# FFN products on h itself from the fourth f-tile on, in place of scale * x with two shift columns

## The chip, the cores and the metric

The kernel runs on one core of one Trainium2 chip. The metric is the device time of one execution in microseconds (us); lower is better. Engines are named as in the profile: PE (matmul), PEld (its weight loads), DVE, ACT, POOL, and SP, which issues DMAs.

## The reference, cut to what matters

The model is a two-layer backbone over 128 context tokens and 256 latent tokens (together T = 384 columns). Each layer has two SwiGLU feed-forward blocks (FFNs) around a token mixer, so there are four FFNs. Width D is 1024, hidden width is 2816.

```
h = modulate(rmsnorm(x, norm_g), shift, scale)      # y * (1 + scale) + shift
x = x + 0.5 * gate * ((silu(h @ wg) * (h @ wu)) @ wd)
```

Shift, scale and gate are vectors of D values, one set for the context tokens and one for the latent ones.

## The kernel before, in words

Activations lie transposed: the 128 partitions hold a slice of the width, the free axis holds the 384 tokens. xT holds x as 8 such slices (k = 0 to 7).

Every product of the FFN is done in three passes (`mm3`): weights and activations are each split into a high part (rounded to fp32r) and a low part (the rest), and high*high, high*low and low*high are added up in one PSUM tile. `loadw` loads a weight tile by a DMA that SP issues, ACT casts the high part wh (L575), DVE subtracts for the low part wl (L576).

`ffn` has two stages. In the gate/up stage a loop over 22 f-tiles (f = 0 to 21) multiplies each of two weight tiles (gate, then up) with the 8 slices of the activation: 2 x 8 x 3 = 48 matmuls for one f-tile. The activation is not h. RMS norm needs the sum of squares over the whole width, and so as not to wait for it, the kernel multiplies with scale * x (tiles xh and xl, written by `norm_step` while the stage before still runs) and appends the two shift vectors as columns 384 and 385. So xh and xl have T + 2 = 386 columns, and each gate/up matmul streams 386. `norm_end` (L560) adds up the squares after f = 0 and forms r, one over the root, on DVE and ACT; r is finished by the DVE instruction on L527. The epilogue of an f-tile (L625 to L634) then copies the two shift columns of the product out of PSUM (L628), multiplies gate and up by r (L629), applies silu with the shift product as bias, once for each token segment (L631), adds the other shift product and multiplies (L632), and writes the high and low part of the result to row f of gh (L633, ACT) and gl (L634, DVE). In the down stage 8 x 22 x 3 matmuls for the 8 output slices read gh and gl with 384 columns, and `residual` adds to xT.

In the first three FFNs some matmuls for the modulation vectors ("fills", L482) stand between the f-tiles; the fourth has none.

The instructions of an engine run in a fixed order, which a planner sets when the kernel is built: at each point it takes, among those it holds to be ready, the one that stands first in the program. Buffers of a pool are reused in turn. The mixer's function `normed` forms h in the same way as the change does (POOL multiplies by r, ACT scales and shifts, ACT casts, DVE subtracts), for the products of the mixer; its helper records everything on L267.

Of the kernel before, what the change touches and what calls it, by code (L numbers as in the profile page):

```python
# [10 lines left out]
F32 = mybir.dt.float32  # L11
F32R = mybir.dt.float32r
AF = mybir.ActivationFunctionType
ALU = mybir.AluOpType
# [3 lines left out]
KD = D // 128  # L18
TP = 128
TS = 256  # L20
T = TP + TS
SEGS = ((0, TP), (TP, T))
DEPTH = 2
DFF = 2816
NF = DFF // 128
# [286 lines left out]
class Kernel:  # L312
# [235 lines left out]
    def norm_step(self, k):  # L548
# [8 lines left out]
        if k:  # L557
            (nc.vector if k == KD - 1 else nc.gpsimd).tensor_tensor(out=self.acc, in0=self.acc, in1=sq, op=ALU.add)

    def norm_end(self):  # L560
        if self.r is not None:
            return
        ps = self.psm()[:, :T]
        self.nc.tensor.matmul(ps, self.k(K_ONE), self.acc, start=True, stop=True)
        self.r = self.rsqrt([ps], [128, T], 1.0 / D, self.eps[:, 0:1], lambda i, n: self.xp.tile([128, T], F32, tag=f"nr{n}", name="nr"))[0]
# [29 lines left out]
    def ffn(self, l, which, mods, nxt):  # L595
        nc, tc, I = self.nc, self.tc, self.I
        sub = 2 * which
        wg, wu, wd = I['ffn_gate'][l, which], I['ffn_up'][l, which], I['ffn_down'][l, which]
        with ExitStack() as st:

            tp = st.enter_context(tc.tile_pool(name="ft", bufs=1, reuse_waits="tile"))
            wp = st.enter_context(tc.tile_pool(name="fw", bufs=FW, reuse_waits="tile"))
            gp = st.enter_context(tc.tile_pool(name="fg", bufs=1, reuse_waits="tile"))
            gh = gp.tile([128, NF, T], F32R, name="gh")
            gl = gp.tile([128, NF, T], F32R, name="gl")
            fills = chain.from_iterable(self.ada(x, i, tp) for x, i in mods)
            steps = (KD + 1) * len(mods)
            if l == sub == 0:
                rest = self.rest(tp)
                next(rest)  # L610
                fills = chain(fills, rest)
                steps += 3
            xh, xl = self.xh, self.xl

            for f in range(NF):
                cols = slice(f * 128, (f + 1) * 128)
                ws = [self.loadw(w[:, cols].rearrange("(k p) f -> p k f", p=128), [128, KD, 128], wp, 1 if f else 4) for w in (wg, wu)]
                gu = [self.psm() for w in ws]

                for i, k in sorted(((i, k) for i in range(2) for k in range(KD)), key=lambda x: f == 0 and x[1] == KD - 1):  # L620
                    self.mm3(gu[i][:, 0:T + 2], ws[i][0][:, k, :], ws[i][1][:, k, :], xh[:, k, :], xl[:, k, :], k == 0, k == KD - 1)
                self.norm_end()
                for _ in range(steps * (f + 1) // NF - steps * f // NF):
                    next(fills, None)
                b = tp.tile([128, 4], F32, tag="fb", bufs=2, name="fb")  # L625
                g, u = (tp.tile([128, T], F32, tag=n, bufs=2, name=n) for n in ("fs", "fa"))
                for i, x in enumerate((g, u)):
                    nc.vector.tensor_copy(out=b[:, 2 * i:2 * i + 2], in_=gu[i][:, T:T + 2])  # L628
                    nc.vector.tensor_mul(out=x, in0=gu[i][:, 0:T], in1=self.r)  # L629
                for c, (x, y) in enumerate(SEGS):  # L630
                    nc.scalar.activation(out=g[:, x:y], in_=g[:, x:y], func=AF.Silu, bias=b[:, c:c + 1])  # L631
                    nc.vector.scalar_tensor_tensor(out=u[:, x:y], in0=u[:, x:y], scalar=b[:, 2 + c:3 + c], in1=g[:, x:y], op0=ALU.add, op1=ALU.mult)  # L632
                nc.scalar.copy(out=gh[:, f, :], in_=u)  # L633
                nc.vector.tensor_sub(out=gl[:, f, :], in0=u, in1=gh[:, f, :])  # L634
            assert next(fills, self) is self
            G = self.adac[l, 3 * sub + 2]
            if nxt:
                self.norm_begin(nxt)
            else:
                self.final_begin()  # L640
            for m in range(KD):
                ps = self.psd()[:, :T]
                for k0 in range(0, NF, KD):
                    n = min(KD, NF - k0)
                    d = self.loadw(wd[k0 * 128:(k0 + n) * 128, m * 128:(m + 1) * 128].rearrange("(k p) f -> p k f", p=128), [128, n, 128], wp)
                    for k in range(n):
                        kk = k0 + k
                        self.mm3(ps, d[0][:, k, :], d[1][:, k, :], gh[:, kk, :], gl[:, kk, :], kk == 0, kk == NF - 1)
                self.residual(m, ps, G)
                (self.norm_step if nxt else self.final_step)(m)  # L650
# [1477 lines left out]
```

## Time and profile before

| | |
|---|---|
| median of 3 runs | 2522.77 us (2519.91 to 2525.49) |
| the profiled execution, its time | 2523.17 us |
| its span, first to last instruction | 2521.4 us |
| PE busy | 2394.0 us (95%) |
| DVE busy | 1581.8 us (63%) |
| ACT busy | 1127.0 us (45%) |
| POOL busy | 489.5 us (19%) |
| granted PE clock, mean | 0.979 of 2.4 GHz |

A row of the timeline gives the start in us from the start of the span, the duration, the engine, the line, the operation, the tile written and the tiles read, and the shapes. Matmul durations overlap; how fast PE goes is the distance from start to start. A row of a stretch gives the busy time of each engine in it, the number of instructions, then the granted clock, the busy share of the DMA engines and GB/s.

### The profile page before, as it was taken

To read this page: it belongs to the slowest core of one execution; us is meant where nothing else is said; L and a number is where in the kernel's file an instruction comes from. 1 tells how busy PE (TensorE), PEld (TensorE's weight loads), DVE (VectorE), ACT (ScalarE), POOL (GpSimd) and SP (SyncE) were. 2 spreads that over 40 slices of the span, in tenths; PEclk is the share of its full clock that TensorE was granted. 3 is DMA by queue.
4 is the path that set the end of the run, shared out by engine and by line. 5 is a ranking of instruction groups with operands and counts; after the bars stand their busy time and mean duration, and the time that the engine had idled before them with its cause. 6 is when DMAs were issued, how large, how long until landed. Compare 5 with 4: busy or idle time off the path is not lost.

```text
span 2521.4 us, 51149 instructions
## 1 busy us (share of the span) xinstructions
PE 2394.0 (95%) x20545; PEld 2168.4 (86%) x20545; DVE 1581.8 (63%) x3466; ACT 1127.0 (45%) x2303; POOL 489.5 (19%) x667
## 2 busy tenths in 40 slices
PE   6999999999999879999999999999999997899998
PEld 4999998778888669999999999978788885799998
DVE  3544468778658886555445544786885587865543
ACT  3333346555446544333343333754544654443332
POOL 3000024323104541000000001441231345210000
PEclk8999999999999989999999999999999998999999
DMA  9876454323355126554557754533333541444442
GB/s 309 270 250 212 121 152 108 82 76 92 92 151 151 51 82 204 170 176 143 160 177 226 220 172 129 142 97 82 84 96 97 142 148 30 146 126 126 125 116 86
DMA packets 501677, 354.31 MB, mean 141 GB/s; under 512 B 40035, under 2 KB 479985, under 8 KB 500927
## 3 DMA queue, kind: packets, MB, share of 16 engines
q1 hardware_dynamic: 496288, 337.44, 45.5%
q0 software_dynamic: 3680, 6.18, 1.2%
q10 hardware_dynamic: 1471, 7.41, 0.8%
q8 instruction: 162, 2.65, 0.4%
q14 instruction: 76, 0.62, 0.1%
HBM read 326.59 MB, written 24.38 MB: 139 GB/s over the span
## 4 chain that ended last, share of the span: by engine, by line
PE 77%; DVE 12%; ACT 3%; issue 3%; POOL 3%; DMA 2%; SPq 0%; ACTq 0%; POOLq 0%; DVEq 0%
PE psd L267 17%; PE psm L267 12%; PE psm L586 10%; PE psm L588 10%; PE psm L587 10%; PE psd L586 5%; PE psd L587 5%; PE psd L588 5%; PE pss L482 3%; DVE wl L267 2%; POOL kb L267 1%; DVE gD L267 1%; DVE M L267 1%; ACT L267 1%; DMA xT<-xd 1%
## 5 line engine op out<-in xcount | busy, mean ns | idle before, releaser
L575 ACT CAST wh<-wraw 128x1024 fp32r<-128x1024 f32 (+2 forms) x296 | 279.9, 956 | 674.4 <-PE psm L587 264.4
L586 PE MATMUL psm<-xh,wh 128*128 128x386 f32 x1408 | 486.1, 345 | 1.0 <-DVE xh L545 0.6
L588 PE MATMUL psm<-xh,wl 128*128 128x386 f32 x1408 | 478.4, 340 | 1.0 <-DVE wl L576 1.0
L587 PE MATMUL psm<-xl,wh 128*128 128x386 f32 x1408 | 478.1, 340 | 0.0
L576 DVE TENSOR_TENSOR wl<-wraw,wh 128x1024 fp32r<-128x1024 f32 (+2 forms) x296 | 325.6, 1106 | 184.6 <-ACT wh L575 184.4
L267 PE MATMUL psd<-mhh,wh 128*128 128x384 f32 x848 | 295.9, 350 | 6.2 <-DVE sb L267 5.4
L267 PE MATMUL psd<-mhl,wh 128*128 128x384 f32 x848 | 297.3, 351 | 2.7 <-DVE mhl L267 2.7
L267 PE MATMUL psd<-mhh,wl 128*128 128x384 f32 x848 | 297.3, 351 | 0.0
L586 PEld LDWEIGHTS psm<-xh,wh 128*128 128x128 f32 x1408 | 266.1, 189 | 27.3 <-issue 16.9
L267 DVE TENSOR_TENSOR wl<-wraw,wh 128x512 fp32r<-128x512 f32 x324 | 244.7, 766 | 70.2 <-ACT wh L267 67.5
L588 PEld LDWEIGHTS psm<-xh,wl 128*128 128x128 f32 x1408 | 265.3, 188 | 2.1 <-DVE wl L576 2.1
L587 PEld LDWEIGHTS psm<-xl,wh 128*128 128x128 f32 x1408 | 266.8, 190 | 0.1
L267 ACT CAST wh<-wraw 128x512 fp32r<-128x512 f32 x324 | 191.7, 615 | 133.8 <-PE psd L267 111.0
L628 DVE COPY fb<-psm 128x2 f32<-128x2 f32 x176 | 27.9, 159 | 343.4 <-PE psm L588 343.4
L587 PE MATMUL psd<-gl,wh 128*128 128x384 f32 x704 | 235.9, 335 | 0.0
L588 PE MATMUL psd<-gh,wl 128*128 128x384 f32 x704 | 235.9, 335 | 0.0
L586 PE MATMUL psd<-gh,wh 128*128 128x384 f32 x704 | 235.6, 335 | 0.0
L267 PEld LDWEIGHTS psd<-mhh,wh 128*128 128x128 f32 x848 | 161.5, 191 | 21.1 <-issue 11.7
L267 PEld LDWEIGHTS psd<-mhl,wh 128*128 128x128 f32 x848 | 161.3, 190 | 14.9 <-issue 5.9
L267 PEld LDWEIGHTS psd<-mhh,wl 128*128 128x128 f32 x848 | 161.4, 190 | 8.8 <-issue 2.4
L267 PE MATMUL psd<-ob,wh 128*128 128x384 f32 x384 | 110.1, 364 | 24.8 <-ACT ob L267 17.3
L586 PEld LDWEIGHTS psd<-gh,wh 128*128 128x128 f32 x704 | 132.2, 188 | 0.9 <-issue 0.4
(434 smaller groups left out, 4297.3 us busy)
## 6 DMA issues: line engine op xcount, KB each, us to landing
wada<-in_w_ada_dram SPq DMA_DIRECT2D x144, 512.0 KB, 4.5
wraw<-in_w_in_dram SPq DMA_DIRECT2D x112, 512.0 KB, 3.9
wraw<-in_ffn_gate_dram SPq DMA_DIRECT2D x88, 512.0 KB, 4.7
wraw<-in_ffn_up_dram SPq DMA_DIRECT2D x88, 512.0 KB, 3.9
wraw<-in_ffn_down_dram SPq DMA_DIRECT2D x64, 512.0 KB, 3.9
wraw<-in_ffn_down_dram SPq DMA_DIRECT2D x32, 384.0 KB, 3.4
gate<-sa SPq DMA_DIRECT2D x48, 192.0 KB, 3.5
gate<-gate SPq DMA_DIRECT2D x48, 192.0 KB, 2.5
```

What stands on the lines that cost most here:

```text
L267: r = f(*a, **k)
L482: nc.tensor.matmul(ps[32 * j:32 * j + 32, 0:256], self.cs[:, kk, :], w[:, 256 * j:256 * j + 256], start=(kk == 0), stop=(kk == KD - 1), ti ...
L575: nc.scalar.copy(out=h[:, x], in_=r[:, x])
L576: nc.vector.tensor_sub(out=lo[:, x], in0=r[:, x], in1=h[:, x])
L586: nc.tensor.matmul(ps, wh, xh, start=first, stop=False)
L587: nc.tensor.matmul(ps, wh, xl, start=False, stop=False)
L588: nc.tensor.matmul(ps, wl, xh, start=False, stop=last)
L628: nc.vector.tensor_copy(out=b[:, 2 * i:2 * i + 2], in_=gu[i][:, T:T + 2])
```

## The change

For f = 0 to 2 the loop is as before. In the epilogues of f = 0 and f = 1 the new function `norm_h` forms h for four slices each: POOL multiplies xT by r into a buffer nu (two buffers), ACT applies scale and shift in place (two instructions, one for each token segment), ACT casts the high part, DVE subtracts for the low part. The results th and tl are put into rows 14 to 21 of gh and gl, which the loop does not write before f = 14. From f = 3 on the matmuls read h with 384 columns: th and tl for f = 3 to 11; from f = 12 on columns 0 to 383 of xh and xl, into which ACT copies one slice of th and tl in each of the epilogues of f = 3 to 10. The epilogue from f = 3 on is a silu straight from PSUM, one multiply, and the two writes of gh and gl.

```diff
+    def norm_h(self, k, pool, hh, hl):
+        nc, (l, sub) = self.nc, self.ls
+        A, S = self.adac[l, 3 * sub + 1], self.adac[l, 3 * sub]
+        u = pool.tile([128, T], F32, tag="nu", bufs=2, name="nu")
+        nc.gpsimd.tensor_mul(out=u, in0=self.xT[:, k, :], in1=self.r)
+        for c, (a, b) in enumerate(SEGS):
+            nc.scalar.activation(out=u[:, a:b], in_=u[:, a:b], func=AF.Identity, scale=A[:, k, c:c + 1], bias=S[:, k, c:c + 1])
+        nc.scalar.copy(out=hh[:, k, :], in_=u)
+        nc.vector.tensor_sub(out=hl[:, k, :], in0=u, in1=hh[:, k, :])
...
-            xh, xl = self.xh, self.xl
+            F1, F2 = 3, 12
+            x, n = (self.xh, self.xl), T + 2
+            th, tl = gh[:, NF - KD:, :], gl[:, NF - KD:, :]
...
+                if f == F1:
+                    x, n = (th, tl), T
+                elif f == F2:
+                    x = self.xh[:, :, 0:T], self.xl[:, :, 0:T]
...
-                    self.mm3(gu[i][:, 0:T + 2], ws[i][0][:, k, :], ws[i][1][:, k, :], xh[:, k, :], xl[:, k, :], k == 0, k == KD - 1)
+                    self.mm3(gu[i][:, 0:n], ws[i][0][:, k, :], ws[i][1][:, k, :], x[0][:, k, :], x[1][:, k, :], k == 0, k == KD - 1)
...
+                if f < F1:
...
+                else:
+                    nc.scalar.activation(out=g, in_=gu[0][:, 0:T], func=AF.Silu)
+                    nc.vector.tensor_mul(out=u, in0=gu[1][:, 0:T], in1=g)
                 nc.scalar.copy(out=gh[:, f, :], in_=u)
                 nc.vector.tensor_sub(out=gl[:, f, :], in0=u, in1=gh[:, f, :])
+                if f < 2:
+                    for k in range(4 * f, 4 * f + 4):
+                        self.norm_h(k, tp, th, tl)
+                elif F1 <= f < F1 + KD:
+                    k = f - F1
+                    nc.scalar.copy(out=self.xh[:, k, 0:T], in_=th[:, k, :])
+                    nc.scalar.copy(out=self.xl[:, k, 0:T], in_=tl[:, k, :])
```

## Rows read from the trace of the kernel before

**Rows 1.** The page: busy time by engine; the chain that ended last, by engine.

```profile
PE 2394.0 (95%) x20545; PEld 2168.4 (86%) x20545; DVE 1581.8 (63%) x3466; ACT 1127.0 (45%) x2303; POOL 489.5 (19%) x667
...
PE 77%; DVE 12%; ACT 3%; issue 3%; POOL 3%; DMA 2%; SPq 0%; ACTq 0%; POOLq 0%; DVEq 0%
```

**Rows 2.** Stretches: gate/up from f = 3 (fourth FFN), f = 2 (first FFN).

```profile
2253.80:2406.60 152.80, 152.80 (x865) 152.80 (x864) 86.81 (x162) 59.67 (x90) 0.00 (x0) 1.00 0.42 124
62.60:262.30 199.70, 199.70 (x1376) 181.38 (x1375) 100.28 (x205) 66.32 (x101) 0.00 (x0) 1.00 0.76 237
```

**Rows 3.** Timeline of PE, gate/up stage of the fourth FFN.

```profile
2330.19 0.34 PE L586 MATMUL psm<-xh,wh 128*128 128x386 f32 x1
...
2332.33 0.34 PE L586 MATMUL psm<-xh,wh 128*128 128x386 f32 x1
...
2333.22 0.33 PE L588 MATMUL psm<-xh,wl 128*128 128x386 f32 x1
...
2334.26 0.34 PE L588 MATMUL psm<-xh,wl 128*128 128x386 f32 x1
```

**Rows 4.** Timeline of PE, down stage of the fourth FFN.

```profile
2452.78 0.33 PE L586 MATMUL psd<-gh,wh 128*128 128x384 f32 x1
...
2454.86 0.33 PE L586 MATMUL psd<-gh,wh 128*128 128x384 f32 x1
```

**Rows 5.** Timeline of DVE: the last instruction that forms r, four FFNs.

```profile
54.05 0.56 DVE L527 SCALAR_TENSOR_TENSOR nr<-nr 128x384 f32<-128x384 f32 x1
...
999.45 0.56 DVE L527 SCALAR_TENSOR_TENSOR nr<-nr 128x384 f32<-128x384 f32 x1
...
1299.42 0.55 DVE L527 SCALAR_TENSOR_TENSOR nr<-nr 128x384 f32<-128x384 f32 x1
...
2240.66 0.56 DVE L527 SCALAR_TENSOR_TENSOR nr<-nr 128x384 f32<-128x384 f32 x1
```

**Rows 6.** Timeline of PE: the first matmul of f = 3, four FFNs.

```profile
72.23 0.44 PE L586 MATMUL psm<-xh,wh 128*128 128x386 f32 x1
...
1014.70 0.45 PE L586 MATMUL psm<-xh,wh 128*128 128x386 f32 x1
...
1314.62 0.44 PE L586 MATMUL psm<-xh,wh 128*128 128x386 f32 x1
...
2253.75 0.34 PE L586 MATMUL psm<-xh,wh 128*128 128x386 f32 x1
```

**Rows 7.** Stretches from r into f = 3: PE, PEld, DVE, ACT, POOL.

```profile
54.61:75.90 21.29, 21.29 (x147) 19.42 (x146) 13.63 (x28) 8.69 (x14) 0.00 (x0) 1.00 1.02 314
1000.01:1018.40 18.39, 18.39 (x113) 17.08 (x113) 11.92 (x23) 9.09 (x14) 0.00 (x0) 1.00 0.75 230
1299.97:1318.30 18.33, 18.33 (x130) 16.50 (x129) 11.45 (x23) 8.45 (x14) 0.00 (x0) 1.00 0.74 227
2241.22:2257.50 16.28, 16.28 (x94) 16.28 (x93) 11.79 (x23) 8.96 (x14) 0.00 (x0) 1.00 0.44 129
```

**Rows 8.** Groups by line (count, busy us, mean ns): mixer's `normed`, write of gh.

```profile
L267 POOL TENSOR_TENSOR nu<-xT,nr 128x384 f32<-128x384 f32 x16 | 18.2, 1150 | 16.6 <-DVE nr L267 14.3 <-DVE mhl L267 2.2
...
L267 DVE TENSOR_TENSOR mhl<-nu,mhh 128x384 fp32r<-128x384 f32 x16 | 12.9, 818 | 0.3
...
L633 ACT CAST gh<-fa 128x384 fp32r<-128x384 f32 x88 | 45.2, 513 | 60.3 <-DVE fa L632 60.2
```

**Rows 9.** Timeline of ACT and POOL in the mixer's `normed`.

```profile
389.17 0.50 ACT L267 CAST mhh<-nu 128x384 fp32r<-128x384 f32 x1
389.57 0.99 ACT L267 ACTIVATE nu<-nu,adac 128x256 f32<-128x256 f32 x2
390.46 0.50 ACT L267 CAST mhh<-nu 128x384 fp32r<-128x384 f32 x1
...
386.12 1.56 POOL L267 TENSOR_TENSOR nu<-xT,nr 128x384 f32<-128x384 f32 x1
```

**Rows 10.** Timeline of ACT in the gate/up stage of the fourth FFN.

```profile
2258.07 1.05 ACT L575 CAST wh<-wraw 128x1024 fp32r<-128x1024 f32 x1 [2.10 <-PE psm L587]
2259.02 0.80 ACT L631 ACTIVATE fs<-fs,fb 128x128 f32<-128x128 f32 x2
2262.31 1.05 ACT L575 CAST wh<-wraw 128x1024 fp32r<-128x1024 f32 x1 [2.49 <-issue]
```

More of the change, by code (lines that the diff above doesn't have):

```diff
@@ L626, in ffn @@
                 g, u = (tp.tile([128, T], F32, tag=n, bufs=2, name=n) for n in ("fs", "fa"))
[L627 to L632, printed above, removed]
+                if f < F1:
+                    for i, y in enumerate((g, u)):
+                        nc.vector.tensor_copy(out=b[:, 2 * i:2 * i + 2], in_=gu[i][:, T:T + 2])
+                        nc.vector.tensor_mul(out=y, in0=gu[i][:, 0:T], in1=self.r)
+                    for c, (p, q) in enumerate(SEGS):
+                        nc.scalar.activation(out=g[:, p:q], in_=g[:, p:q], func=AF.Silu, bias=b[:, c:c + 1])
+                        nc.vector.scalar_tensor_tensor(out=u[:, p:q], in0=u[:, p:q], scalar=b[:, 2 + c:3 + c], in1=g[:, p:q], op0=ALU.add, op1=ALU.mult)
+                else:
+                    nc.scalar.activation(out=g, in_=gu[0][:, 0:T], func=AF.Silu)
+                    nc.vector.tensor_mul(out=u, in0=gu[1][:, 0:T], in1=g)
                 nc.scalar.copy(out=gh[:, f, :], in_=u)
                 nc.vector.tensor_sub(out=gl[:, f, :], in0=u, in1=gh[:, f, :])
+                if f < 2:
[5 more added lines that the diff above has]
+                    nc.scalar.copy(out=self.xl[:, k, 0:T], in_=tl[:, k, :])
             assert next(fills, self) is self
```

## The prediction

> **What bounds the kernel now.** I read the page first: PE is busy 95% of the span, and the chain that ended last lies on PE for 77% [rows 1]. Then the stretches of the gate/up stage, which the change touches: from f = 3 on PE is busy in every microsecond, while DVE and ACT are at 57% and 39% in the fourth FFN and POOL does nothing [rows 2]. So the stage is worth what PE's matmuls cost, and work taken from DVE or ACT there is worth nothing by itself. Third, the timeline of PE for the distance from start to start. The 18 f-tiles from f = 3 to 20 of the fourth FFN are 864 matmuls in 152.80 us [rows 2], 176.9 ns each with 386 columns; 12 in a row in the down stage, with 384 columns out of gh and gl, take 2.08 us [rows 4], 173.3 ns each. The granted clock is 1.00, 2.4 GHz, in the whole stage [rows 2], and no start is late in either. The difference, 3.5 ns, is what the change can win on a matmul.
>
> Last, the way from r to f = 3, because there the new work must fit in. r is finished at 54.61, 1000.01, 1299.97 and 2241.22 us (start plus duration [rows 5]); f = 3 starts at 72.23, 1014.70, 1314.62 and 2253.75 [rows 6].
>
> **What it removes: columns.** From f = 3 on there are 19 f-tiles x 48 matmuls x 4 FFNs = 3648 matmuls with 384 columns in place of 386. They fall into two parts.
>
> f = 3 to 11: 9 x 48 x 4 = 1728 matmuls. They read rows 14 to 21 of gh and gl, the very places that the down stage reads at 173.3 ns. 1728 x 3.5 ns = 6.1 us. I take this as nearly certain as a rate.
>
> f = 12 to 21: 10 x 48 x 4 = 1920 matmuls. They have 384 columns but read xh and xl, whose slices lie 386 columns apart. The trace of before has no such matmul. The bounds: two columns less at 2.4 GHz, 0.83 ns, gives 1.6 us; the whole difference, 3.5 ns, gives 6.8 us. Which is nearer? With 386 columns the distance is not constant inside an f-tile: from 2330.19 to 2332.33 twelve starts take 178.3 ns each, from 2333.22 to 2334.26 six take 173.3 ns [rows 3]. If 386 columns can go as fast as 384, the loss is tied to the place that is read more than to the number of columns, and the places stay. I take 1.5 ns, nearer the lower bound: 2.9 us. Together 9.0 us won, with bounds of 7.7 and 12.9.
>
> The Trainium skill has a rule that speaks against the change: its page "TensorE: Matmul & The Clock Gate", section "Wait — 56ns, not 53.3ns?", puts the distance of matmuls at the full clock at the columns over 2.4 GHz and a fixed 2.5 ns or so. By that rule 386 and 384 columns would differ by 0.83 ns. The trace's two levels differ by four times that, and neither is the rule's 163 ns, so the measurement decides; but the two levels are of different tiles, and the rule would be right if place and stage made the rest.
>
> **What it removes: the epilogue.** From f = 3 on two PSUM copies, one of two multiplies by r, the segment-wise silu and two multiply-adds go or shrink. All of this is on DVE and ACT behind PE, which idles for none of it [rows 2]: nothing won. The silu straight from PSUM and the one multiply are not longer than what they replace. If this cover were gone, the last f-tile's epilogue would show; its row of gh is read 63 matmuls into the down stage, 10.9 us later.
>
> **What it adds and moves: forming h.** Per FFN eight times: one POOL multiply, two ACT instructions and an ACT cast, one DVE subtraction. The mixer does the same with the same shapes. ACT takes 1.29 us a slice when it does them without a pause (cast to cast [rows 9]), POOL 1.15 us, DVE 0.82 us in the mean [rows 8]. POOL is idle there [rows 7], and no DMA of the stage waits behind it.
>
> All of it hangs on r, and the matmuls of f = 3 need the last slice after 21 of their 24 first-product matmuls, 21 x 173.3 ns = 3.64 us after their start. So the time for it is 75.87 - 54.61 = 21.26 us in the first FFN, and 18.33, 18.29 and 16.17 us in the others. The work: 8 x 1.29 = 10.32 us of ACT, before it one POOL multiply (1.15), behind it one DVE subtraction (0.82): 12.29 us. And ACT already has 8.69, 9.09, 8.45 and 8.96 us of work in these windows [rows 7]. Sums: 20.98, 21.38, 20.74, 21.25. Against the time there is, that is 0 (0.3 to spare), 3.05, 2.45 and 5.08 us too much: 10.6 us in all, in which PE stands, since every later matmul is behind these.
>
> The bounds of this. From below: some of ACT's work of f = 2 can come after (silu 0.80, one cast of a weight tile 1.05 [rows 10], the cast for gh 0.51 [rows 8]; 2.36 us). Then 0, 0.69, 0.09 and 2.72 are left, 3.5 us. From above: with two buffers nu, slice k + 2 can't start before slice k is subtracted; with a POOL multiply that is slowed to 1.56 us [rows 9], 1.29 and 0.82, two slices take at least 3.67 us, 1.84 each; the pauses of 0.55 us, seven times, are 3.8 us for each FFN if nothing fills them: 3.5, 6.85, 6.25 and 8.9, 25.5 us. I take the middle value, 10.6: ACT has other work to put into the pauses, but not always the right one at the right time.
>
> The copies back into xh and xl are 16 casts of 0.51 us for each FFN, 8 us of ACT over eight f-tiles of 8.5 us; ACT has 61% free there [rows 2]. Nothing, as long as no weight cast is late behind one: a cast starts when its buffer is free, at 2258.07 and 2262.31 [rows 10], each 4.2 us before its matmuls, takes 1.05 us, and can wait for two copies. The two writes into rows 14 to 21 from f = 14 on follow the last reading of these rows by two f-tiles: no wait.
>
> **The sum.** The profiled execution took 2523.17 us, 0.4 us above the median of the runs. 2523.17 - 9.0 + 10.6 = 2524.8 us. About 0.2%, 5.0 us, is what a measurement of this kernel can tell from no change, so this is no change: the stall at f = 3 eats what the columns give.
>
> **The rivals.**
>
> *The stall is small and the columns win* (faster). ACT's order lets the eight slices go first and puts f = 2's rest behind them: 3.5 us of stall against 9.0 to 12.9 us: 2517.7 to 2513.8 us, say 2516. For it: POOL is free, and ACT's work of f = 2 isn't urgent. Against it: the window of the fourth FFN is too short even so.
>
> *ACT holds back the weight casts* (slower). `norm_h` for slices 0 to 3 stands ahead of f = 1's loads in the program, and for 4 to 7 ahead of f = 2's. Where both are ready, the planner puts the slices first, and the casts of f = 2's second and f = 3's first weight tile queue behind them on ACT. DVE's subtraction for wl waits for the cast, and PE for both. A cast has 4.2 us; once it is put back by more than about 2 us (4.2 less 1.05 and DVE's subtraction) PE stands. That is the upper bound, 25.5 us, against 9.0: 2539.7; with three quarters of it 2533. It ends above 2523 as soon as the stall is over 9.0 us. Against it: slices must wait for POOL and for a buffer, and then a cast gets in.
>
> *The columns are worth only their number* (slower). The 3.5 ns belongs to the stage and not to the tiles: 3648 x 0.83 ns = 3.0 us won, with 10.6 us of stall 2530.8. For it: gate/up and down have a different mix of work on DVE and ACT beside them. Against it: the fast and slow stretches inside an f-tile [rows 3] lie 1 us apart, and the down stage has casts and subtractions too, at a steady 173.3 ns. By the rule of the Trainium skill's page "TensorE: Matmul & The Clock Gate" cited above it would come out just so.
>
> **Chances.** No change, near 2524.8: 0.42. Faster, near 2516: 0.30. Slower by the casts: 0.18; slower by the columns: 0.10. So faster by over 0.2% 0.30, within 0.2% 0.42, slower 0.28. The likeliest case alone has 2518 to 2528. The range of 8 in 10 goes from 2513, where the least stall meets the most gain (2523.2 - 12.9 + 3.5 = 2513.8), to 2536, which holds the columns' case and the better half of the casts'.
>
> **What would show it.** In the timeline of PE: 173 ns from start to start for f = 3 to 11; a value between 173 and 176 ns for f = 12 to 21; and in the first f-tiles a gap of 2 to 5 us, none or little in the first FFN and most in the fourth, before a matmul on h whose releaser is DVE (tl) or ACT. If the gap stands before f = 2's second product or f = 3's first matmul instead, released by L575 or L576, the casts were held back. In the stretch from r to f = 3 ACT should be busy nearly throughout. The prediction is wrong if f = 3 starts without a gap, if f = 3 to 11 stays at 177 ns, or if f = 12 to 21 goes at 173 ns with little stall, which together is the faster case.

## The result, and the profile after

The changed kernel is slower, by half a percent. Its median is 2535.3 us (2533.21 to 2542.91, 6 runs) against 2522.5 us for the kernel before in the same session (6 runs): ratio 1.0052, 95% interval 1.0035 to 1.0068. The time lies inside the predicted range, but not in the likeliest case. The profiled execution took 2533.21 us, its span is 2531.1 us.

In the page of the changed kernel PE is as busy as in [rows 1], DVE less, ACT a little more; in the second line, the chain that ended last, PE has two points less, DVE and ACT one more each.

```profile
PE 2398.1 (95%) x20545; PEld 2169.2 (86%) x20545; DVE 1503.6 (59%) x3118; ACT 1163.3 (46%) x2387; POOL 523.7 (21%) x699
...
PE 75%; DVE 13%; ACT 4%; issue 3%; POOL 3%; DMA 1%; SPq 0%; ACTq 0%; POOLq 0%; DVEq 0%
```

**The columns came.** The stretches of the fourth FFN's gate/up stage of the changed kernel, f = 4 to 11 and f = 12 to 20 (columns: length; PE, PEld, DVE, ACT, POOL busy with instructions; granted clock; DMA share; GB/s), answer to [rows 2]:

```profile
2273.06:2339.66 66.60, 66.60 (x386) 66.60 (x385) 27.82 (x32) 26.02 (x40) 0.00 (x0) 1.00 0.44 129
2339.66:2415.52 75.86, 75.86 (x434) 75.86 (x433) 31.26 (x36) 26.20 (x36) 0.00 (x0) 1.00 0.42 124
```

The stretches hold 8 x 48 = 384 and 9 x 48 = 432 matmuls (the counts take in two at the edges): 173.4 and 175.6 ns each, where [rows 2] gave 176.9. PE is never idle in them and the clock is 1.00.

**The loss is ahead of them.** The f-tiles after r, same view and columns: f = 1 and f = 2 of the first FFN, f = 2 of the second, f = 2 and f = 3 of the third and of the fourth:

```profile
50.70:65.90 15.20, 12.05 (x96) 9.95 (x92) 10.23 (x24) 11.10 (x24) 5.98 (x6) 0.99 1.05 338
65.90:78.10 12.20, 12.17 (x54) 10.93 (x55) 8.31 (x10) 9.76 (x19) 2.07 (x3) 0.73 0.86 276
1008.20:1019.30 11.10, 10.58 (x78) 9.32 (x74) 7.49 (x17) 10.46 (x25) 6.05 (x6) 1.00 0.32 97
1305.60:1322.20 16.60, 12.22 (x88) 9.82 (x84) 12.64 (x28) 14.96 (x33) 6.04 (x6) 0.88 0.49 173
1322.20:1332.70 10.50, 10.50 (x58) 9.23 (x58) 3.94 (x4) 8.29 (x19) 0.00 (x0) 0.86 0.70 211
2249.70:2261.90 12.20, 8.65 (x50) 8.33 (x49) 8.54 (x18) 11.23 (x26) 6.10 (x6) 0.94 0.15 44
2261.90:2273.10 11.20, 10.83 (x48) 10.33 (x49) 6.40 (x8) 9.12 (x19) 0.00 (x0) 0.76 0.49 143
```

Two things are to be seen. PE stands: length less PE's busy time is 3.15, 0.03, 0.52, 4.38, 0, 3.55 and 0.37 us, 12.0 us in all. And where it has stood for 2 us and more, or just after, the granted clock is 0.73 to 0.94; in the kernel before it was 1.00 from r to f = 3 in all four FFNs [rows 7]. (1 - clock) x length is 3.3, 2.0, 1.5, 0.7 and 2.7 us in the five stretches below 0.99, 10.2 us at most, since part of the low clock falls into the standing time.

The timeline of PE shows both in one place, at the end of f = 2 and the start of f = 3 of the fourth FFN (last column: idle time before, and what ended it):

```profile
2258.01 0.34 PE L599 MATMUL psm<-xh,wl 128*128 128x386 f32 x1
2261.90 0.69 PE L597 MATMUL psm<-gh,wh 128*128 128x384 f32 x1 [3.55 <-ACT wh L586]
2262.38 0.52 PE L598 MATMUL psm<-gl,wh 128*128 128x384 f32 x1
2263.27 0.69 PE L599 MATMUL psm<-gh,wl 128*128 128x384 f32 x1 [0.37 <-DVE wl L587]
...
2264.07 0.52 PE L598 MATMUL psm<-gl,wh 128*128 128x384 f32 x1
2264.39 0.52 PE L599 MATMUL psm<-gh,wl 128*128 128x384 f32 x1
```

and the stretch just after, columns as above:

```profile
2262.00:2267.00 5.00, 4.63 (x14) 4.13 (x15) 4.13 (x7) 5.00 (x10) 0.00 (x0) 0.50 0.36 105
```

f = 3 doesn't wait for h. It waits for L586, the cast of a weight tile. Then, at a granted clock of 0.50, the lower level (1.2 GHz), its matmuls take 0.52 to 0.69 us in place of 0.33 and start 0.32 us apart in place of 0.17. ACT's timeline says why the cast is late:

```profile
2245.51 1.05 ACT L586 CAST wh<-wraw 128x1024 fp32r<-128x1024 f32 x1 [2.09 <-PE psm L598]
...
2249.97 0.51 ACT L568 CAST gh<-nu 128x384 fp32r<-128x384 f32 x1
2250.38 0.98 ACT L567 ACTIVATE nu<-nu,adac 128x128 f32<-128x128 f32 x2
...
2252.68 0.99 ACT L567 ACTIVATE nu<-nu,adac 128x128 f32<-128x128 f32 x2 [0.61 <-POOL nu L565]
...
2259.93 0.98 ACT L567 ACTIVATE nu<-nu,adac 128x128 f32<-128x128 f32 x2
2260.81 1.03 ACT L586 CAST wh<-wraw 128x1024 fp32r<-128x1024 f32 x1
```

Between 2246.56 and 2260.81 no weight tile is cast; the work on seven slices (L567, L568) and ACT's part of the epilogues of f = 0 to 2 stand in between. Before, one came every 4.2 us [rows 10]. The waits of this place (2249 to 2275; us in total, times, longest) name the same cast, and POOL, which waits for the subtraction that gives it a buffer nu back:

```profile
POOL nu L565 <- DVE gl L569: 7.9, 6, 3.8
...
PE psm L597 <- ACT wh L586: 3.6, 1, 3.6
```

In the first and the third FFN the longest wait is another one. There a matmul of the fills waits for DVE, and not for a cast: PE in the first FFN, then PE and DVE in the third.

```profile
64.92 0.59 PE L482 MATMUL pss<-wada,cs 128*32 128x256 f32 x2 [2.04 <-DVE gl L569]
...
1319.72 0.69 PE L494 MATMUL pss<-kt,adaev 128*128 128x128 f32 x2 [3.53 <-DVE adaev L488]
...
1316.39 0.85 DVE L569 TENSOR_TENSOR gl<-nu,gh 128x384 fp32r<-128x384 f32 x1 [0.64 <-ACT gh L568]
...
1318.79 0.55 DVE L569 TENSOR_TENSOR gl<-nu,gh 128x384 fp32r<-128x384 f32 x1
1319.25 0.41 DVE L488 COPY adaev<-pss 128x256 f32<-128x256 f32 x1
```

In the first it is a slice's subtraction (L569) that lets the matmul go; in the third DVE's copy for the fills (L488) stands in DVE's order behind the subtractions of two slices and an epilogue. Of the 12.0 us of standing, 4.9 end with the cast of a weight tile or the subtraction after it (3.55 and 0.37 in the fourth FFN, 0.52 in the second, 0.42 in the first). The other 7.1 stand ahead of the fills' matmuls: 2.75 in the first FFN and 3.53 in the third for DVE, and 0.85 in the third for the fills' own matmul before.

**Where the 12.8 us went.** From the first to the last matmul of gate/up the four FFNs take 222.6, 205.4, 216.2 and 188.3 us before, 832.5 us in all; after, 226.7, 203.7, 221.0 and 193.1, 844.5 us, 12.0 more. Columns: 1728 x (177.0 - 173.5) + 1920 x (177.0 - 175.6) = 8.7 us less. So the first f-tiles lost 12.0 + 8.7 = 20.7 us: 12.0 standing, and by difference 8.7 at the lower clock, which the 10.2 us above have room for.

### The profile page after: what moved, and what is told of

Same layout as the page of the kernel before. It is cut to its first block, busy times and chain, and to the rows that moved or that the text cites. A ratio compares the mean times of both kernels' runs of the same rounds, so it can differ in the third digit from the quotient of the medians.

```text
span 2531.1 us, 50948 instructions
## 1 busy us (share of the span) xinstructions
PE 2398.1 (95%) x20545; PEld 2169.2 (86%) x20545; DVE 1503.6 (59%) x3118; ACT 1163.3 (46%) x2387; POOL 523.7 (21%) x699
## 4 chain that ended last, share of the span: by engine, by line
PE 75%; DVE 13%; ACT 4%; issue 3%; POOL 3%; DMA 1%; SPq 0%; ACTq 0%; POOLq 0%; DVEq 0%
PE psd L267 17%; PE psm L267 12%; PE psm L597 10%; PE psm L599 9%; PE psm L598 9%; PE psd L597 5%; PE psd L599 5%; PE psd L598 5%; PE pss L482 3%; DVE wl L267 2%; POOL kb L267 1%; DVE gD L267 1%; DVE M L267 1%; DVE t L267 1%; ACT wh L267 1%
## 5 line engine op out<-in xcount | busy, mean ns | idle before, releaser
L586 ACT CAST wh<-wraw 128x1024 fp32r<-128x1024 f32 (+2 forms) x296 | 279.7, 955 | 698.0 <-issue 497.4
L597 PE MATMUL psm<-xh,wh 128*128 128x384 f32 (+1 forms) x832 | 286.7, 345 | 1.1 <-ACT wh L586 1.1
L599 PE MATMUL psm<-xh,wl 128*128 128x384 f32 (+1 forms) x832 | 283.4, 341 | 1.6 <-DVE wl L587 1.6
L598 PE MATMUL psm<-xl,wh 128*128 128x384 f32 (+1 forms) x832 | 283.0, 340 | 0.0
L597 PE MATMUL psm<-gh,wh 128*128 128x384 f32 x576 | 196.6, 341 | 4.1 <-ACT wh L586 4.1
L599 PE MATMUL psm<-gh,wl 128*128 128x384 f32 x576 | 194.0, 337 | 0.4 <-DVE wl L587 0.4
L598 PE MATMUL psm<-gl,wh 128*128 128x384 f32 x576 | 193.9, 337 | 0.0
L597 PEld LDWEIGHTS psm<-xh,wh 128*128 128x128 f32 x832 | 157.9, 190 | 16.0 <-issue 9.1
L599 PEld LDWEIGHTS psm<-xh,wl 128*128 128x128 f32 x832 | 157.5, 189 | 3.9 <-DVE wl L587 2.7
L598 PEld LDWEIGHTS psm<-xl,wh 128*128 128x128 f32 x832 | 157.8, 190 | 0.1
```

Of the source, the lines that this page charges most:

```text
L586: nc.scalar.copy(out=h[:, x], in_=r[:, x])
L597: nc.tensor.matmul(ps, wh, xh, start=first, stop=False)
L598: nc.tensor.matmul(ps, wh, xl, start=False, stop=False)
L599: nc.tensor.matmul(ps, wl, xh, start=False, stop=last)
```

## The experiments

The sum of the four gate/up stages accounts for the times to within 4 us (e7_cols400, one run: 7 us):

| kernel | gate/up, us (less before's 832.5) | median, us (less before's in its session) | ratio, 95% |
| --- | --- | --- | --- |
| changed | 844.5 (+12.0) | 2535.3 (+12.8) | 1.0035 to 1.0068 |
| e1_pad | 838.9 (+6.4) | 2527.98 (+6.1) | 1.0020 to 1.0045 |
| e2_noform | 826.7 (-5.8) | 2516.6 (-5.2) | 0.9972 to 0.9990 |
| e3_order | 837.1 (+4.6) | 2528.91 (+7.1) | 1.0020 to 1.0045 |
| e4_spread | 830.3 (-2.2) | 2523.65 (+1.8) | 0.9995 to 1.0016 |
| e5_contig | 846.2 (+13.7) | 2537.02 (+14.4) | 1.0037 to 1.0063 |
| e6_nu3 | 833.9 (+1.4) | 2523.54 (+0.9) | 0.9990 to 1.0008 |
| e7_cols400 | 856.9 (+24.4) | 2554.38 (+31.7), one run | |
| e8_best | 829.8 (-2.7) | 2520.34 (-2.3) | 0.9982 to 1.0000 |
| e9_start | 841.7 (+9.2) | 2533.81 (+10.8) | 1.0030 to 1.0055 |
| e10_best | 826.7 (-5.8) | 2516.65 (-6.4) | 0.9964 to 0.9983 |

What differs between the two columns lies in the mixers and the down stages: in the profiled executions of these kernels the span without the four gate/up stages is 1682.9 to 1695.8 us.

**e1_pad.** The kernel before, with the room of a slice widened:

```diff
-        self.xh = xp.tile([128, KD, T + 2], F32R, tag="xh", name="xh")
+        self.xh = xp.tile([128, KD, 400], F32R, tag="xh", name="xh")[:, :, 0:T + 2]
```

and xl the same.

> The kernel before with one edit: the slices of xh and xl lie 400 columns apart in place of 386, of which 386 are used as before. Theory of the place (what slows a product of 386 columns is where its slice starts): all 4224 gate/up matmuls go at about 174.2 ns from start to start in place of 177.0, 12 us less, about 2511 us. Rival (the number of columns does it): 177 ns as before and no change, 2522.5 us.

The 864 matmuls of f = 3 to 20 of the fourth FFN of e1_pad, by the stretch:

```profile
2256.60:2411.16 154.56, 154.56 (x865) 154.56 (x865) 86.88 (x162) 59.68 (x90) 0.00 (x0) 1.00 0.42 122
```

178.9 ns, more than the 176.9 of before: slices whose starts are all alike don't make 386 columns fast. The number of columns costs something too (384 columns at the same starts: e5_contig).

**e2_noform.** The changed kernel without `norm_h` and the copies; from f = 3 on columns 0 to 383 of xh and xl are read, so that shift and r are left out there.

```diff
-                    x, n = (th, tl), T
+                    x, n = (self.xh[:, :, 0:T], self.xl[:, :, 0:T]), T
...
-                if f < 2:
-                    for k in range(4 * f, 4 * f + 4):
-                        self.norm_h(k, tp, th, tl)
```

> The changed kernel without norm_h and without the copies back: from f = 3 on the products read columns 0 to 383 of xh and xl as they are, so h is not formed and the shift is left out there. It shows what the columns give without what forming h costs. Theory (the whole stall comes from forming h, and the rate is set by the place): no gap at f = 2 or f = 3, 175.5 ns from f = 3 on, 3648 x 1.4 = 5 us less than before, 2517 us. Rival (the short distance at f = 3 to 11 comes from the lighter stage, not from the tiles gh and gl): 173.4 ns from f = 3 on, 13 us less, 2510 us.

The same 864 matmuls in e2_noform:

```profile
2245.80:2397.52 151.72, 151.72 (x867) 151.72 (x866) 63.32 (x75) 52.30 (x72) 0.00 (x0) 1.00 0.43 125
```

175.6 ns at once from f = 3, and no f-tile is longer than before. 3648 x 1.4 = 5.1 us won, 5.8 in the sum of the stages, 5.2 in the median. So two columns less out of xh are worth 1.4 ns wherever they stand, the shorter epilogue gives and costs nothing more, and all of the loss comes with forming h and copying it, which this run leaves out together.

**e3_order.** The changed kernel, with the weight tiles of f = 1 to 4 put ahead in the planner's order:

```diff
-                ws = [self.loadw(...) for w in (wg, wu)]
+                with (tc.high_priority() if 1 <= f <= 4 else ExitStack()):
+                    ws = [self.loadw(...) for w in (wg, wu)]
```

> The changed kernel, only the order is changed: the loads of the weight tiles of f = 1 to 4, their casts and subtractions go ahead of norm_h's slices in the planner's order. Theory A (casts held back by the slices): most of the stall of 24 us at f = 1 to 3 goes, under 8 us is left, about 2518 us. Theory B (ACT, POOL and DVE can't have eight slices ready by f = 3 in any order): the gap moves to the first matmul on h and is released by DVE's subtraction of a slice; 10 us or more are left, 2525 us or more.

f = 2 and f = 3 of the fourth FFN of e3_order, and the waits there (2249 to 2272):

```profile
2249.70:2258.20 8.50, 8.50 (x50) 8.50 (x49) 7.63 (x14) 7.96 (x18) 2.25 (x2) 1.00 0.43 124
2258.20:2270.00 11.80, 9.92 (x51) 8.14 (x50) 7.52 (x13) 10.11 (x22) 4.27 (x4) 1.00 0.31 90
```

```profile
POOL nu L565 <- DVE gl L569: 10.0, 6, 4.4
...
PEld psm L597 <- ACT gh L568: 1.9, 2, 1.2
PEld psm L598 <- DVE gl L569: 1.8, 4, 0.7
```

The stall of f = 2 is gone, in the third FFN too (10.13 us, before 10.13, in the changed kernel 16.66), so the order made it. A smaller one is now at f = 3, and its releasers are the slices (L568, L569), as the prediction had it: with the casts in time h itself is late. It comes in many short waits, the clock stays at 1.00 in every stretch that is longer than before, and the loss ahead of the columns' gain falls from 20.7 to 4.6 + 8.7 = 13.3 us. The difference, 7.4 us, is near the 8.7 that the lower clock had cost: PE loses about as much by waiting as the changed kernel's 12.0 us, in shorter pieces. Of the 13.3 us 7.3 are idle time of PE; the rest are starts that come late while the matmul ahead still counts as busy. No run changes the clock alone, so its share is worked out and not shown by itself. Part of the 13.3 us is the edit's own doing: with the casts ahead r is finished later after the start of its stage than in the changed kernel, by 3.1, 0.7, 2.2 and 0.7 us in the four FFNs, and every slice starts from r. No run here separates that from ACT's lack of time.

**e4_spread.** Two slices in each of f = 0 to 3 in place of four in f = 0 and 1; h is read from f = 5 on, the copies from f = 13 on:

```diff
-            F1, F2 = 3, 12
+            F1, F2 = 5, 13
...
-                if f < 2:
-                    for k in range(4 * f, 4 * f + 4):
+                if f < 4:
+                    for k in range(2 * f, 2 * f + 2):
```

> The changed kernel with two slices in each of the epilogues of f = 0 to 3 in place of four in f = 0 and 1; h is read from f = 5 on, xh and xl again from f = 13. The columns of two f-tiles in each FFN are given up, 2 x 48 x 4 x 3.5 ns = 1.3 us. Theory A (order): the slices still stand ahead of the casts, but fewer at a time; about half of the stall is left, 12 us, 2524 us. Theory B (too little time up to f = 3): the window is longer by two f-tiles, 17 us, no stall is left, 2515 us.

f = 2 to 4 of the fourth FFN of e4_spread:

```profile
2251.00:2276.50 25.50, 25.50 (x146) 25.50 (x145) 19.82 (x36) 21.83 (x45) 7.22 (x6) 1.00 0.43 126
```

PE is busy throughout: given five f-tiles, the same eight slices cost nothing there, with the order as the change has it. The first FFN still loses 4.1 us over f = 0 to 3 (f = 1 takes 13.88 us, before 10.12; f = 2 10.96, before 9.70), where PE waits once 1.7 us for a cast (L586) and 0.7 us for the fills' copy (L488); f = 4 of the third takes 11.30 us, before 10.34. A late r is not the reason: it is finished 2.2 us after the start of f = 1 in the first FFN and 3.8 to 5.2 us after it in the others. The stages are 2.2 us shorter; the median shows no change.

**e6_nu3.** e3_order with a third buffer:

```diff
-        u = pool.tile([128, T], F32, tag="nu", bufs=2, name="nu")
+        u = pool.tile([128, T], F32, tag="nu", bufs=3, name="nu")
```

> The kernel of e3_order with a third buffer nu. Theory C (with the casts ahead, what is late are the slices, because a slice waits for the subtraction two slices before it to give its buffer back): the gaps at f = 3 shrink from some 3.2 us an FFN to 1 us or less, about 2521 us. Rival D (ACT itself has no time for the slices): the gaps stay, 2529 us.

f = 3 takes 10.95 us in the first FFN (e3_order 12.74), 10.70 in the second (12.29) and 10.71 in the third (11.35), so the buffer was part of it; in the fourth it takes 11.98 (11.76). The rows of the fourth, stretch and first wait of PE in it:

```profile
2254.10:2266.10 12.00, 10.48 (x50) 9.78 (x50) 7.94 (x14) 9.79 (x22) 3.19 (x3) 0.86 0.31 89
```

```profile
2257.86 0.61 PE L597 MATMUL psm<-gh,wh 128*128 128x384 f32 x2 [1.51 <-ACT gh L568]
```

The waits became one of 1.5 us, and the clock fell to 0.86 over the stretch: less standing, paid back in clock. The expected 2521 us was too little: 2523.54 came, no change from before.

**e5_contig, e7_cols400, e9_start: what a matmul's distance hangs on.** e5_contig packs the copies 384 columns apart, e9_start moves them on by 8 columns; e7_cols400 streams 400 columns in e1_pad.

```diff
+            ch, cl = (t.rearrange("p k t -> p (k t)")[:, 0:KD * T].rearrange("p (k t) -> p k t", t=T) for t in (self.xh, self.xl))
...
-                    x = self.xh[:, :, 0:T], self.xl[:, :, 0:T]
+                    x = ch, cl
```

```diff
-            ... [:, 0:KD * T] ...
+            ... [:, 8:8 + KD * T] ...
```

```diff
-                    self.mm3(gu[i][:, 0:T + 2], ...)
+                    self.mm3(gu[i][:, 0:400], ...)
```

> The changed kernel, only the copies of f = 3 to 10 put the slices 384 columns apart into the room of xh and xl in place of 386, and f = 12 on reads them there. Theory (384 columns whose slices start 384 apart go at 173.4 ns in whatever tile): f = 12 to 21 go at 173.4 ns in place of 175.5, 1920 x 2.1 = 4.0 us less than the changed kernel, 2531 us; the stalls stay. Rival (the short distance at f = 3 to 11 belongs to gh and gl): 175.5 ns stays, 2535 us.

> The kernel of e1_pad, but all 400 columns of a slice are streamed (14 more columns, filled with xT, whose products nobody reads; they are added work). Theory (the time of a matmul goes in steps of 16 columns, so that the two columns past 384 cost nearly a whole step): about 180 ns from one matmul's start to the next, like the 178.9 of 386 columns. Rival (each column counts): 178.9 + 14 x 0.42 = 184.7 ns.

> The kernel of e5_contig, only that the eight slices begin 8 columns (32 bytes) further into the room of xh and xl, so that a slice starts at a multiple of 64 bytes as those of gh and gl do (in e5_contig they start 32 bytes past one). Theory (what is left between 175.6 and 173.4 ns is where a slice starts): f = 12 to 21 go at 173.4 ns, 1920 x 2.1 = 4.0 us less than e5_contig, 2533 us or a little less; the stalls stay. Rival (it is something else about the tiles xh and xl, such as where in the memory they lie: the products of the mixer with mhh and mhl, which also start 32 bytes past a multiple of 64, go at 173.8 ns in the kernel before): 175.6 ns stays, 2537 us.

f = 12 to 20 of e5_contig, f = 3 to 20 of e7_cols400 and f = 12 to 20 of e9_start, fourth FFN:

```profile
2345.22:2421.08 75.86, 75.86 (x434) 75.86 (x434) 31.27 (x36) 26.20 (x36) 0.00 (x0) 1.00 0.42 124
```

```profile
2279.39:2437.30 157.91, 157.91 (x865) 157.91 (x865) 86.87 (x162) 59.70 (x90) 0.00 (x0) 1.00 0.41 120
```

```profile
2339.93:2414.82 74.89, 74.89 (x434) 74.89 (x434) 31.27 (x36) 26.20 (x36) 0.00 (x0) 1.00 0.44 126
```

e5_contig: 175.6 ns, as with slices 386 apart; the distance of the slices is not it. e9_start: 173.4 ns, with the same distance, tile, stage and columns; where the slices start is it. In the built program xh begins 32 bytes past a multiple of 64, gh and gl at one. e7_cols400: 182.8 ns, between what the two theories gave (180 and 184.7), so the time doesn't go in steps of 16 columns, nor does each column cost the same: from 384 (e5_contig) to 386 (e1_pad), with all starts 32 bytes past a multiple of 64, it is 3.3 ns for two columns, from there to 400 it is 3.9 ns for fourteen.

**e8_best and e10_best: the edits together.** e8_best is e4_spread with the casts of f = 1 to 6 ahead and e5_contig's copies. e10_best has e9_start's copies in its place, and forms h later in the first FFN alone:

```diff
-            F1, F2 = 5, 13
+            F0, F1, F2 = (2, 7, 14) if l == sub == 0 else (0, 5, 13)
+            J = 2 if F0 else 1
...
-                if f < 4:
-                    for k in range(2 * f, 2 * f + 2):
+                if F0 <= f < F0 + 4:
+                    for k in range(2 * (f - F0), 2 * (f - F0) + 2):
```

with J slices copied in an f-tile; in the first FFN the loads of f = 1 to 8 go ahead.

> The three edits together: the loads of f = 1 to 6 ahead in the planner's order, two slices in each of f = 0 to 3 (h is read from f = 5 on), and the copies 384 columns apart. Theory (the stalls go with the order and the time, the columns are worth what e2 and the tiles f = 3 to 11 showed): 17 x 48 x 4 = 3264 matmuls 3.6 ns shorter, 11.8 us, and no stall but 1 to 3 us in the first FFN: about 2512 us. Rival (the time that PE gains in gate and up is lost again after it): 2520 us or more.

> The kernel of e8_best with the start of e9_start, and the first FFN alone later: its slices are formed two in each of f = 2 to 5, h is read from f = 7 on, copied two slices an f-tile, and the copies are read from f = 14 on. Theory (gate and up set the time, the first FFN lost some 4 us in e8_best because r is late there): three FFNs x 17 x 48 x 3.6 ns = 8.8 us and one of 15 x 48 x 3.6 = 2.6 us (with e9_start's theory; with its rival 1.5 ns in place of 3.6 from f = 13 and 14 on, 3.6 us less), less 1.5 us that the third FFN loses at f = 4: about 2513 us, by the rival 2517 us. Rival (the first FFN loses the same wherever its slices are formed): 2517 to 2520 us.

e8_best misses its 2512 us, with 2520.34: its copies go at 175.6 ns (e5_contig), and the first FFN still takes 223.8 us. e10_best is the one kernel that computes the whole and is clearly faster than both: 2516.65 us, 0.17 to 0.36% below before. f = 5 to 20 of its fourth FFN:

```profile
2261.24:2394.40 133.16, 133.16 (x770) 133.16 (x770) 56.45 (x67) 52.02 (x79) 0.00 (x0) 1.00 0.44 127
```

768 matmuls at 173.4 ns. It expected 2513: its columns are worth 17 x 48 x 3 x 3.6 + 15 x 48 x 3.6 = 11.4 us, and 5.8 came. Of the missing 5.6 us 3.2 are in the first FFN (223.2 us; 222.6 - 2.6 would be 220.0) and 1.5 in f = 4 of the third, 11.68 us long, where a matmul of the fills waits for adaev and starts 1.46 us after the one ahead of it. Forming the first FFN's slices later won nothing: against before, without the columns' gain (2.0 and 2.6 us), that stage loses 3.1 us in e8_best and 3.1 in e10_best, as the rival had it. Nor is a late r what sets that FFN apart: in e8_best r is finished 6.9 us after the start of f = 1 in the first FFN and 7.4 in the third. What costs the 3.1 us stays open.

## Why the prediction was right in its range and wrong in its likeliest case

The range, 2513 to 2536 us, holds 2535.3 near its end; the likeliest case, no change near 2524.8, did not come. That the range holds is in part luck, since the term for forming h was about half of what came and one part of it, the clock, stood in no rival's sum.

*Columns, 9.0 us: right.* 8.7 us came. f = 3 to 11 gave 3.5 ns a matmul as said, and f = 12 to 21 gave 1.4 where 1.5 was taken. The reason for the second was only half right. It was taken that the loss belongs to the place that is read, by the distance of the slices. It does belong to the place, though by where a slice starts (e9_start against e5_contig, 2.2 ns), and the number counts as well (e2_noform, 1.4 ns; e1_pad against e5_contig, 3.3 ns). The rule of the Trainium skill's page "TensorE: Matmul & The Clock Gate", section "Wait — 56ns, not 53.3ns?", gives 0.83 ns for two columns. The trace does not agree: two columns are worth 1.4 and 3.3 ns in the pairs above, and the rival built on the columns' number alone fell.

*Epilogue, nothing: right.* e2_noform, which has it without the forming, gains what its columns are worth.

*Forming h, 10.6 us: the step that failed.* The loss is 20.7 us. The step counted ACT's work from r to f = 3 and let PE stand for what didn't fit, before a matmul on h. Two things were otherwise. First, the place: the slices went ahead of other work in the queues, and no long wait of PE was for h. On ACT they went ahead of the weight casts, and in the fourth FFN PE stood 3.55 us at the first matmul of f = 3 for L586. That is the rival "ACT holds back the weight casts" (0.18), which gave 2533 to 2539.7; 2535.3 came. But its mechanism ends only 4.9 of the 12.0 us of standing, the other 7.1 stand ahead of the fills' matmuls, and its price was worked out from the pauses of two buffers, without a clock; that its number fits is luck. e3_order shows that the order makes this place, and also that h itself can be late: with the casts ahead 13.3 us are still lost, some 9 of them at f = 3 of the last three FFNs in waits that the slices release (part of that because r was later, too). Second, the term for the clock was missing. PE's standing time is 12.0 us, near the 10.6 of the account, and that is luck as well: by FFN it is 3.2, 0.5, 4.4 and 3.9 us where the account had 0, 3.05, 2.45 and 5.08, and it ends with other work than h. The other 8.7 us, by difference, are matmuls that ran at the lower clock after it. In the fourth FFN 3.55 us of standing are followed by an f = 3 that takes 11.25 us in place of 8.32.

*By FFN.* Said was none in the first and most in the fourth. With a quarter of the columns' gain, 2.2 us, added to what each grew by, the four FFNs lost 6.3, 0.5, 7.0 and 7.0 us. In the first and third the fills' matmuls stand in PE's order between the f-tiles and wait for DVE, whose copies for them stand behind slices and epilogues. The account left them out.

*Two buffers nu, the upper bound's mechanism: seen.* POOL waits for L569 7.9 us in the fourth FFN; added to e3_order, a third buffer took part of the loss at f = 3 away in three FFNs. It was not tried on the changed kernel itself.

*Copies, nothing: right.* 16 casts of 0.51 us an FFN; from f = 4 on PE isn't idle in any FFN.

## What to carry to other kernels

When new work goes onto an engine that feeds the bound engine, ask first what its queue will put behind the new work, for every one that waits on that queue: here the weight casts on ACT and the fills' copies on DVE. Two slices an f-tile, wanted only from f = 5 on, cost nothing in the second FFN and 0.5 us, in f = 0, in the fourth (e4_spread); four an f-tile, wanted at f = 3, cost 20.7 us over the four. Price a stall of TensorE with the slower matmuls behind it: here they were by difference four tenths of the loss, and in e3_order a loss of 13.3 us in short pieces kept the clock. Before counting columns, look at where the operand's rows start; moving them by 32 bytes was worth 2.2 ns a matmul, two columns less out of xh 1.4.

## What the runs showed of the hardware that was not expected

- Where PE stood for 2 to 4 us at a stretch, matmuls after it ran at the lower level: granted clock 0.50 from 2262 to 2267 us, 0.76 over f = 3 of the fourth FFN, 0.73 over f = 2 of the first. In e3_order, with 13.3 us lost in waits of at most 1.6 us, it was 1.00 in every f-tile that grew. In e6_nu3 one wait of 1.51 us, with weight loads standing 1.8 us, went with 0.86; the length of a wait alone doesn't decide it, and what does stays open.
- 384 columns go at 173.4 ns when the slices start at a multiple of 64 bytes (gh and gl, and e9_start) and at 175.6 when they start 32 bytes past one (e5_contig). It is not the whole rule: the mixer's products with mhh and mhl also start 32 bytes past one, and go at 173.8 ns on the mean. Nor does it hold slice by slice: from f = 12 on the changed kernel's slices start 32, 40, 48, 56, 0, 8, 16 and 24 bytes past a multiple of 64 and take 174.0, 177.2, 176.3, 175.0, 173.6, 178.9, 174.2 and 175.2 ns (fourth FFN), so the one at a multiple is the fastest, but the one 32 past is hardly slower. What differs there stays open.
- With 386 columns the distance repeats by slice: in the kernel before, in the fourth FFN, a matmul takes 178.3, 180.0, 176.7, 178.9, 176.4, 176.7, 175.0 and 173.6 ns for the eight slices, the same within 0.1 ns in both products and in f = 5 to 10 and f = 14 to 20. That is what [rows 3] showed as a fast and a slow stretch.
